# Attention's first keys and queries on two queues, one load per query tile, and Fourier weights in a work tile

## The chip, the core and the metric

The kernel runs on one core of a Trainium2 chip. The core has five engines, each with its own instruction queue: TensorE (PE, matmuls; the profile lists its weight loads as PEld), VectorE (DVE), ScalarE (ACT), GpSimd (POOL) and SyncE (SP). Instructions of one queue run in the order in which they are written there, and wait on semaphores for the other engines. DMAs are issued by SP, ACT or POOL. The metric is the device time of one execution in microseconds; lower is better.

## What is computed

The reference is a backbone of two layers on 2048 latent tokens and a prefix of 256 context tokens, 1024 wide. Each layer is one input projection that feeds four groups, and one output projection:

```python
hp = (rmsnorm(x, g) * (1 + scale) + shift) @ w_in
q  = (rmsnorm(hp[q]) @ w_uq) -> 4 heads x (64 plain + 32 rotary)
kn, kr, v = kv(hp[kv])           # kr: 32 rotary rows, shared by the 4 heads
s    = einsum("bqhd,bkhd->bhqk", q, concat(kn, kr)) / sqrt(96)
attn = softmax(s) @ v            # latents read latents and context: 2304 keys
four = real(fft2(hp[f], over tokens and within a group)) @ w_fourier + b_fourier
conv = conv_module(hp[c]);  sgu = spatial_gating(hp[s])
x = x + gate * (concat(attn, conv, four, sgu) * silu(hp[gate])) @ w_out
```

Context tokens go through the same weights in the first layer and give only keys and values in the second.

## The kernel before

Matmuls are done on fp32 data split into a high and a low part (names that end in h and l), so that one product is three matmuls: high x high (line 286), low x high (287), high x low (288). Keys and queries are kept in DRAM as such pairs between the stages.

A layer has three stages. **Phase A** projects the inputs, superblock by superblock of 768 tokens, each with its weights streamed through a ring (`ring<-wst`). `tm_a` makes the queries: `project()` computes two blocks of 128 plain rows and one block of 128 rotary rows of all heads, and `put` (line 522) splits each into two tiles called `th` and stores them on POOL. There are six `th` tiles, so the third put after one takes its tiles again. The Fourier branch is a generator that phase A advances a step at a time; it starts in the third superblock, multiplies the channel DFT by the weights `wf` (line 824), and reads its input `f` back from DRAM (`fx<-f`). Its weight tile came from its own pool, `fst`. Other short results live in three work tiles called `co`.

**Attention** works on two heads at a time over tiles of 256 queries. Its key tiles have 96 partitions: 64 plain rows of a head and the 32 shared rotary rows. `k0h`, `k0l` are those of the first head of a pair, `k1h`, `k1l` of the second, loaded in three chunks of 512, 768 and 1024 keys, with the plain and the rotary rows in a DMA each. A query tile `qh` or `ql` has 96 partitions too, filled by three DMAs. A score (`s<-k0h,qh`) is a 96-row matmul of 512 keys, in one of eight PSUM banks called s, t and o; DVE takes the maximum over the keys, ACT the exponential `e` (line 1014, with a table load first), and PE transposes `e` and multiplies it by `v`. **The output projection** follows.

The order of instructions on each engine is settled ahead by a scheduler; a load's place is that of its line in the program among the other instructions of its queue. Before attention, the program writes: the first query tiles of both heads on POOL, head 0's keys on POOL and head 1's on SP, the second query tiles on SP, and v on SP.

Of the kernel before, what the change touches and what calls it, by code (L numbers as in the profile page):

```python
# [16 lines left out]
F32 = mybir.dt.float32  # L17
# [7 lines left out]
P = 128  # L25
# [173 lines left out]
class Kern:  # L199
# [401 lines left out]
    def tm_a(self, l, seg, h, w, W, S):  # L601
        nc, A = self.nc, self.A
        t0, bw, cl0 = seg
        nt = bw // P
        lat = t0 < T
        full = not (l == L - 1 and not lat)
        c0 = 0 if full else 32
        kr = self.sq()[:, 0:96].rearrange("p (a b) -> p a b", b=32)
        held, cs = [], []

        def turn(t, cn):
            if t == 0:
                held.extend(self.bank("hold") for _ in range(2))
            for c in range(2):
                nc.tensor.transpose(held[c][:, t * P:(t + 1) * P], cn[:, c * P:(c + 1) * P], self.ident)
            if t == nt - 1:
                for c in range(2):
                    ch, cl = self.x("th", bw, F32R), self.x("th", bw, F32R)
                    self.split(held[c][:, :bw], ch, cl)
                    cs.append((ch, cl))  # L620
                self.later(LP, project)

        def key(krr):
            pk = self.bank("pj")
            for t in range(nt):
                nc.tensor.transpose(pk[0:32, t * P:(t + 1) * P], krr[:, t, :], self.ident)
            self.put(pk[0:32, :bw], [[(slice(0, 32), S["kr" + q][:, t0:t0 + bw])] for q in "hl"])

        def proj(m):
            ps = self.bank("pj")  # L630
            ms = slice(m * P, (m + 1) * P)
            self.mm3(ps[:, :bw], [(W["uq"][k][0][:, ms], W["uq"][k][1][:, ms], cs[k][0], cs[k][1])
                                  for k in range(2)])
            return ps[:, :bw]

        def project():
            for m in range(2):
                self.put(proj(m), [[(slice(0, P), S["q" + q][m * P:(m + 1) * P, t0:t0 + bw])] for q in "hl"])
            pr = proj(2)
            if lat:  # L640
                cos, sin, rot = (self.x("co", bw) for _ in range(3))
                nc.gpsimd.dma_start(out=cos, in_=A["cosq"][:, t0:t0 + bw])
                nc.gpsimd.dma_start(out=sin, in_=A["sinq"][:, t0:t0 + bw])
                for a, b in ((slice(0, 64), slice(64, P)), (slice(64, P), slice(0, 64))):
                    nc.scalar.copy(out=rot[b], in_=pr[a])
                nc.vector.tensor_tensor(cos, pr, cos, op=ALU.mult)
                nc.vector.tensor_tensor(rot, rot, sin, op=ALU.mult)
                nc.vector.tensor_tensor(cos, cos, rot, op=ALU.add)
                pr = cos
            self.put(pr, [[(slice(0, P), S["qr" + q][:, t0:t0 + bw])] for q in "hl"])  # L650

        for t in range(nt):
            ps = self.bank("mm")
            hs = slice(cl0 + t * P, cl0 + (t + 1) * P)
            self.mm3(ps[:, c0:288], [(h[k][0][:, hs], h[k][1][:, hs], w[k][0][:, c0:288], w[k][1][:, c0:288])
                                     for k in range(KT)])
            self.tick()
            nc.scalar.copy(out=kr[:, t], in_=ps[:, 256:288])
            if full:
                sq, ss, r, cn = self.junk(), self.st(), self.st(), self.sq()  # L660
                nc.scalar.activation(out=sq, in_=ps[:, 0:256], func=AF.Square, accum_out=ss[:, 0:1])
                nc.vector.tensor_scalar(ss[:, 1:2], ss[:, 0:1], 1.0 / 256, RMS_EPS, op0=ALU.mult, op1=ALU.add)
                self.rpow(r[:, :1], ss[:, 1:2])
                nc.vector.tensor_scalar(cn, ps[:, 0:256], r[:, 0:1], None, op0=ALU.mult)
                self.later(LT, lambda t=t, cn=cn: turn(t, cn))
        if lat:
            tb = self.sq().rearrange("p (a b c) -> p a b c", a=2, c=32)
            g0 = t0 // P
            nc.gpsimd.dma_start(out=tb[:, 0, :nt], in_=A["cosk"][:, g0:g0 + nt])
            nc.gpsimd.dma_start(out=tb[:, 1, :nt], in_=A["sink"][:, g0:g0 + nt])  # L670
            nc.vector.tensor_tensor(tb[:, 0, :nt], kr[:, :nt], tb[:, 0, :nt], op=ALU.mult)
            for a, b in ((slice(0, 16), slice(16, 32)), (slice(16, 32), slice(0, 16))):
                nc.vector.tensor_tensor(tb[:, 1, :nt, b], kr[:, :nt, a], tb[:, 1, :nt, b], op=ALU.mult)
            nc.vector.tensor_tensor(tb[:, 0, :nt], tb[:, 0, :nt], tb[:, 1, :nt], op=ALU.add)
            krr = tb[:, 0]
        else:
            krr = kr
        self.later(LT + 1, lambda: key(krr))
# [57 lines left out]
    def phase_a(self, l, xsrc, S, hcur, h0, lp, conv, w):  # L736
# [6 lines left out]
        for i, sb in enumerate(SBS):  # L743
# [20 lines left out]
            for ci, name in enumerate(CM_ORDER[i]):  # L764
                w = self.load_w(A["winC"][l, CM.index(name)], 256, lp)
                for seg in cmb:
                    self.lastseg = seg is cmb[-1]
                    self.cm(name, seg, hcur, w, S, M)
                if ci == 0 and i < 2:
                    hnext = self.norm_alloc((self.ap, h0)[i])  # L770
                    self.norm_sb(l, SBS[i + 1], xsrc, hnext)
                if ci == 0 and i == 2:
                    while self.dq:
                        self.tick()
                    self.h1x.__exit__(None, None, None)
                    self.npx.__exit__(None, None, None)
                    fx = self.pool(f"F{l}", "right")
                    steps = self.fourier(l, S, fx.__enter__())
                    self.every = lambda: [next(steps, None) for _ in range(2 if l < L - 1 else 3)]
                if name == "c1":  # L780
                    conv.avail(first + n if i < 2 else NTOK)
# [8 lines left out]
        self.ringx.__exit__(None, None, None)  # L790


    def fourier(self, l, S, p):


        nc, A, v = self.nc, self.A, self.v
# [4 lines left out]
        def T_(tag, shape, dt=F32, bufs=1):  # L801
            return self.t(p, tag, shape, dt, bufs)

        wf = T_("fst", [P, 512], bufs=2).rearrange("p (a b) -> p a b", b=256)
        nc.gpsimd.dma_start(out=wf, in_=A["wf"][l])
        altr, altc = T_("altr", [P, 512]), T_("altc", [P, 1])
        nc.gpsimd.dma_start(out=altr, in_=A["altr"].broadcast_to([P, 512]))
        nc.gpsimd.dma_start(out=altc, in_=A["altc"])
# [153 lines left out]
            yield  # L962


    def load_k(self, S, pool, pr):

        out = []
        for q in range(2):
            h = 2 * pr + q
            kk = [self.t(pool, f"k{q}{part}", [96, NTOK], F32R) for part in "hl"]  # L970
            for a, b in ((0, 512), (512, 1280), (1280, NTOK)):
                s = slice(a, b)
                for part, k in zip("hl", kk):
                    eng = self.nc.gpsimd if h == 0 else self.nc.sync
                    eng.dma_start(out=k[0:64, s].bitcast(F32), in_=S["k" + part][64 * h:64 * h + 64, s])
                    eng.dma_start(out=k[64:96, s].bitcast(F32), in_=S["kr" + part][:, s])
            out.append(kk)
        return out

    def load_q(self, S, pool, h, q0, eng):  # L980
        out = []
        for part in "hl":
            q = self.t(pool, "q" + part, [96, 256], F32R, 4)
            s = slice(q0, q0 + 256)
            eng.dma_start(out=q[0:64].bitcast(F32), in_=S["q" + part][64 * h:64 * h + 64, s])
            for a in range(2):
                r = slice(64 * a + 16 * h, 64 * a + 16 * h + 16)
                eng.dma_start(out=q[64 + 16 * a:80 + 16 * a].bitcast(F32), in_=S["qr" + part][r, s])
            out.append(q)
        return out  # L990

# [251 lines left out]

    def scratch(self, l):
        return {n: self.dr.tile(shape, F32, name=f"{n}{l}") for n, shape in (
            ("kh", [256, NTOK]), ("kl", [256, NTOK]), ("qh", [256, NTOK]), ("ql", [256, NTOK]),
            ("krh", [32, NTOK]), ("krl", [32, NTOK]), ("qrh", [P, NTOK]), ("qrl", [P, NTOK]),
            ("v", [P, NTOK // P, 256]), ("glu", [256, NTOK]), ("dw", [256, NTOK]), ("f", [256, NTOK]),
            ("ys", [256, NTOK]), ("g", [768, NTOK]), ("att", [256, NTOK]), ("conv", [256, NTOK]),
            ("four", [256, NTOK]))}  # L1250
# [1 line left out]
    def build(self):  # L1252
        tc, nc, A = self.tc, self.nc, self.A
        with ExitStack() as es:
# [37 lines left out]
            for l in range(L):  # L1292
# [11 lines left out]
                with self.pool(f"V{l}", "right") as vp:  # L1304
                    vt = self.t(vp, "v", [P, NTOK // P, 256])
                    k0 = self.pool(f"K0_{l}", "left")
                    k0p = k0.__enter__()
                    q0 = [self.load_q(S, k0p, q, 0, nc.gpsimd) for q in range(2)]
                    keys = self.load_k(S, k0p, 0)
                    q1 = [self.load_q(S, k0p, q, 256 if last else T, nc.sync) for q in range(2)]  # L1310
                    nc.sync.dma_start(out=vt, in_=S["v"][:, :, :])
                    self.psum(s=5, t=2, o=1)
                    nc.scalar.activation(out=self.st()[:, 0:1], in_=self.mhalf[:, 0:1], func=AF.Exp)
# [202 lines left out]
```

## Time and profile before

| what | us |
|---|---|
| three runs | 2959.75, 2963.6 (median), 2967.0 |
| the profiled execution | 2965.82 |
| its span, first to last instruction | 2963.8 |
| busy: PE, DVE, ACT, POOL | 2829.0, 1956.1, 1206.9, 569.2 |
| mean granted clock of PE, of full speed | 0.975 |

PE is busy in 95% of the span, so its idle stretches are few and each has a name. A busy time is not a bound by itself: matmuls at half clock count as busy too. In the views "idle before" is the time in which the engine stood just before an instruction, with what ended it.

### The profile page before, as it was taken

To read this page: it belongs to the slowest core of one execution; us is meant where nothing else is said; L and a number is where in the kernel's file an instruction comes from. 1 tells how busy PE (TensorE), PEld (TensorE's weight loads), DVE (VectorE), ACT (ScalarE), POOL (GpSimd) and SP (SyncE) were. 2 spreads that over 40 slices of the span, in tenths; PEclk is the share of its full clock that TensorE was granted. 3 is DMA by queue.
4 is the path that set the end of the run, shared out by engine and by line. 5 is a ranking of instruction groups with operands and counts; after the bars stand their busy time and mean duration, and the time that the engine had idled before them with its cause. 6 is when DMAs were issued, how large, how long until landed. Compare 5 with 4: busy or idle time off the path is not lost. (4 is left out here: it accounts for less than half of the span.)

```text
span 2963.8 us, 50552 instructions
## 1 busy us (share of the span) xinstructions
PE 2829.0 (95%) x18434; PEld 2429.3 (82%) x18434; DVE 1956.1 (66%) x4301; ACT 1206.9 (41%) x3228; POOL 569.2 (19%) x951
## 2 busy tenths in 40 slices
PE   6999999999699999999999999999979999999998
PEld 4889999899567777769998899998767777776998
DVE  5578488485377777654553695894827777775554
ACT  3432343433344454543322343343425455554432
POOL 2301311421211111112322212113321110011210
PEclk8999999999799999999999999999989999999999
DMA  7465343433521010016543443444453101000653
GB/s 244 139 194 177 107 132 106 161 123 117 163 56 29 29 48 25 21 30 207 182 153 117 157 158 105 137 136 139 148 164 93 33 22 45 18 28 15 187 155 110
DMA packets 221849, 326.75 MB, mean 110 GB/s; under 512 B 33456, under 2 KB 152752, under 8 KB 220832
## 3 DMA queue, kind: packets, MB, share of 16 engines
q1 hardware_dynamic: 191392, 240.66, 26.9%
q0 software_dynamic: 29776, 82.83, 8.3%
q8 instruction: 145, 2.38, 0.3%
q14 instruction: 104, 0.85, 0.1%
q10 hardware_dynamic: 432, 0.04, 0.0%
HBM read 232.30 MB, written 91.10 MB: 109 GB/s over the span
## 5 line engine op out<-in xcount | busy, mean ns | idle before, releaser
L1005 DVE TENSOR_REDUCE st<-s 128x1 f32<-128x512 f32 (+1 forms) x636 | 384.9, 631 | 184.4 <-PE s L288 182.6
L1014 ACT ACTIVATE e<-s,st 128x512 f32<-128x512 f32 (+1 forms) x636 | 399.4, 646 | 236.9 <-DVE st L1009 228.3
L286 PE MATMUL mm<-hh,ring 128*128 128x384 f32 (+1 forms) x1408 | 491.4, 349 | 0.0
L287 PE MATMUL mm<-hl,ring 128*128 128x384 f32 (+1 forms) x1408 | 484.7, 344 | 0.0
L288 PE MATMUL mm<-hh,ring 128*128 128x384 f32 (+1 forms) x1408 | 484.1, 344 | 0.0
L1451 DVE SCALAR_TENSOR_TENSOR acc<-win,c_cw,acc 128x384 f32<-128x384 f32 (+5 forms) x780 | 428.4, 572 | 7.4
L1035 PE MATMUL t<-ident,e 128*128 128x128 f32 x2320 | 341.8, 278 | 3.5 <-DVE et L1038 1.9
L1028 PE MATMUL o<-et,v 128*64 128x256 f32 x2320 | 343.7, 392 | 0.0
L1035 PEld LDWEIGHTS t<-ident,e 128*128 128x128 f32 x2320 | 259.7, 141 | 94.9 <-issue 43.7
L1038 DVE COPY et<-t 128x512 f32<-128x512 f32 x377 | 257.9, 686 | 92.1 <-PE t L1035 86.1
L286 PE MATMUL mm<-yh,woh 128*128 128x256 f32 x1040 | 297.2, 286 | 5.2 <-DVE xn L1223 3.7
L288 PE MATMUL mm<-yh,wol 128*128 128x256 f32 x1040 | 293.9, 283 | 0.2 <-DVE wol L278 0.2
L287 PE MATMUL mm<-yl,woh 128*128 128x256 f32 x1040 | 293.8, 282 | 0.1
L286 PEld LDWEIGHTS mm<-hh,ring 128*128 128x128 f32 x1408 | 267.8, 190 | 19.4 <-issue 9.5
L277 ACT CAST ring<-wst 128x256 fp32r<-128x256 f32 (+2 forms) x480 | 184.1, 418 | 240.2 <-DMA wst<-winC 125.4
L287 PEld LDWEIGHTS mm<-hl,ring 128*128 128x128 f32 x1408 | 267.9, 190 | 5.9
L288 PEld LDWEIGHTS mm<-hh,ring 128*128 128x128 f32 x1408 | 267.3, 190 | 5.8
L278 DVE TENSOR_TENSOR ring<-wst,ring 128x256 fp32r<-128x256 f32 (+2 forms) x480 | 201.2, 451 | 74.6 <-ACT ring L277 60.1
L1040 ACT COPY et<-t 128x512 f32<-128x512 f32 x203 | 119.1, 588 | 317.8 <-PE t L1035 317.6
L1028 PEld LDWEIGHTS o<-et,v 128*64 128x64 f32 x2320 | 153.1, 136 | 99.0 <-issue 51.9
L286 PEld LDWEIGHTS mm<-yh,woh 128*128 128x128 f32 x1040 | 198.4, 191 | 6.9 <-DVE xn L1223 4.3
L287 PEld LDWEIGHTS mm<-yl,woh 128*128 128x128 f32 x1040 | 198.3, 191 | 0.4 <-DVE yl L278 0.4
(319 smaller groups left out, 5284.8 us busy)
## 6 DMA issues: line engine op xcount, KB each, us to landing
wst<-winC SPq DMA_DIRECT2D x192, 256.0 KB, 3.1
ast<-wada SPq DMA_DIRECT2D x32, 512.0 KB, 4.5
gt<-g SPq DMA_DIRECT2D x102, 128.0 KB, 3.0
g<-co POOLq DMA_DIRECT2D x60, 192.0 KB, 2.2
wst<-winB SPq DMA_DIRECT2D x24, 384.0 KB, 3.4
x<-xn POOLq DMA_DIRECT2D x72, 128.0 KB, 2.8
ast<-wada SPq DMA_DIRECT2D x8, 1024.0 KB, 9.6
fst<-ft SPq DMA_DIRECT2D x32, 256.0 KB, 3.2
```

The lines of the kernel that those rows point to most:

```text
L277: a = self.nc.scalar.copy(out=hi, in_=src)
L278: b = self.nc.vector.tensor_tensor(lo, src, hi.bitcast(F32), op=ALU.subtract)
L286: mm(out, lhsT=lh, rhs=rh, start=start and i == 0, stop=False)
L287: mm(out, lhsT=lh, rhs=rl, start=False, stop=False)
L288: self.last = mm(out, lhsT=ll, rhs=rh, start=False, stop=stop and i == n - 1)
L1005: self.red = nc.vector.reduce_max(mx[:, i:i + 1], ps[:, :w], axis=AX.X)
L1014: nc.scalar.activation(out=e, in_=ps, func=AF.Exp, bias=nb[:, 0:1], accum_out=sm[:, i:i + 1])
L1028: nc.tensor.matmul(job.o[64 * q:64 * q + 64, 0:256], lhsT=vt[:, g, 64 * h:64 * h + 64], rhs=et[:, 256 * q:256 * q + 256], start=kt == 0, s ...
L1035: nc.tensor.transpose(ps[:, j * P:(j + 1) * P], job.es[j][kt], self.ident)
L1038: nc.vector.tensor_copy(et, ps)
L1040: nc.scalar.copy(out=et, in_=ps)
L1451: eng.scalar_tensor_tensor(ac, win[:, t:t + w], v["cw"][:, l, c, t:t + 1], ac, op0=ALU.mult, op1=ALU.add)
```

## The change

Queries are laid out in DRAM by head, 96 rows each, so that one DMA fills a query tile; the store of a rotary block becomes two DMAs per part, and the store of a plain block has a target of 2 x 64 rows. `load_k` and `load_q` take a list of queues: head 0's first query tile and its keys go with the high part on SP and the low part on ACT; head 1's first query tile and the second query tiles of both heads go on POOL. `wf` is loaded into a `co` tile ahead of the drain of the queued steps, not into the `fst` tile inside the generator.

```diff
 # tm_a, project()
-                self.put(proj(m), [[(slice(0, P), S["q" + q][m * P:(m + 1) * P, t0:t0 + bw])] for q in "hl"])
+                self.put(proj(m), [[(slice(0, P), S["q" + q][2 * m:2 * m + 2, 0:64, t0:t0 + bw])] for q in "hl"])
...
-            self.put(pr, [[(slice(0, P), S["qr" + q][:, t0:t0 + bw])] for q in "hl"])
+            self.put(pr, [[(slice(64 * a, 64 * a + 64), S["q" + q][:, 64 + 16 * a:80 + 16 * a, t0:t0 + bw])
+                           for a in range(2)] for q in "hl"])
 # phase_a
                 if ci == 0 and i == 2:
+                    wf = self.x("co", 512).rearrange("p (a b) -> p a b", b=256)
+                    self.nc.gpsimd.dma_start(out=wf, in_=A["wf"][l])
                     while self.dq:
                         self.tick()
...
-                    steps = self.fourier(l, S, fx.__enter__())
+                    steps = self.fourier(l, S, fx.__enter__(), wf)
 # fourier
-        wf = T_("fst", [P, 512], bufs=2).rearrange("p (a b) -> p a b", b=256)
-        nc.gpsimd.dma_start(out=wf, in_=A["wf"][l])
 # load_k
-                for part, k in zip("hl", kk):
-                    eng = self.nc.gpsimd if h == 0 else self.nc.sync
-                    eng.dma_start(out=k[0:64, s].bitcast(F32), in_=S["k" + part][64 * h:64 * h + 64, s])
-                    eng.dma_start(out=k[64:96, s].bitcast(F32), in_=S["kr" + part][:, s])
+                for i, part in enumerate("hl"):
+                    eng = engs[i] if engs else self.nc.sync
+                    eng.dma_start(out=kk[q][i][0:64, s].bitcast(F32), in_=S["k" + part][64 * h:64 * h + 64, s])
+                    eng.dma_start(out=kk[q][i][64:96, s].bitcast(F32), in_=S["kr" + part][:, s])
+            engs = None
 # load_q
-            eng.dma_start(out=q[0:64].bitcast(F32), in_=S["q" + part][64 * h:64 * h + 64, s])
-            for a in range(2):
-                r = slice(64 * a + 16 * h, 64 * a + 16 * h + 16)
-                eng.dma_start(out=q[64 + 16 * a:80 + 16 * a].bitcast(F32), in_=S["qr" + part][r, s])
+            engs[i % len(engs)].dma_start(out=q.bitcast(F32), in_=S["q" + part][h, :, q0:q0 + 256])
 # the layer's loop
-                    q0 = [self.load_q(S, k0p, q, 0, nc.gpsimd) for q in range(2)]
-                    keys = self.load_k(S, k0p, 0)
-                    q1 = [self.load_q(S, k0p, q, 256 if last else T, nc.sync) for q in range(2)]
+                    q0 = [self.load_q(S, k0p, q, 0, *((nc.sync, nc.scalar), (nc.gpsimd,))[q]) for q in range(2)]
+                    keys = self.load_k(S, k0p, 0, (nc.sync, nc.scalar))
+                    q1 = [self.load_q(S, k0p, q, 256 if last else T, nc.gpsimd) for q in range(2)]
```

Three places in the order of instructions show what moves. On SP at the end of layer 0's phase A, `four` is the last Fourier store of phase A; before, head 1's keys follow it.

```order
258 L961 DMA four_110<-fb_7604 128x256
259 L961 DMA four_110<-fb_7672 128x256
260 L975 DMA k1h_7829<-kh_94 64x512
261 L976 DMA k1h_7829<-krh_98 32x512
262 L975 DMA k1l_7830<-kl_95 64x512
```

With the change, seven rows stand ahead of them there.

```order
260 L984 DMA qh_7811<-qh_96 96x256
261 L975 DMA k0h_7819<-kh_94 64x512
262 L976 DMA k0h_7819<-krh_98 32x512
263 L975 DMA k0h_7819<-kh_94 64x768
264 L976 DMA k0h_7819<-krh_98 32x768
265 L975 DMA k0h_7819<-kh_94 64x1024
266 L976 DMA k0h_7819<-krh_98 32x1024
267 L975 DMA k1h_7821<-kh_94 64x512
268 L976 DMA k1h_7821<-krh_98 32x512
```

On ACT at the same place, the row of `co<-mm` is the activation of phase A's last matmul and the table load is that of the exponential; before, the table load follows directly. With the change, the low part of the first query tile and of the keys stands between.

```order
562 L720 ACTIVATE co_7797<-mm_7772 128x384
563 L984 DMA ql_7813<-ql_97 96x256
564 L975 DMA k0l_7820<-kl_95 64x512
565 L976 DMA k0l_7820<-krl_99 32x512
566 L975 DMA k0l_7820<-kl_95 64x768
567 L976 DMA k0l_7820<-krl_99 32x768
568 L975 DMA k0l_7820<-kl_95 64x1024
569 L976 DMA k0l_7820<-krl_99 32x1024
570 L1010 ACT_TABLE_LOAD
```

On POOL in layer 1's third superblock, before, the load of `wf` comes behind the last block's stores.

```order
747 L522 DMA qh_17353<-th_22758 128x256
748 L522 DMA ql_17354<-th_22759 128x256
749 L722 DMA f_17362<-co_22787 128x512
750 L522 DMA qrh_17357<-th_22781 128x256
751 L522 DMA qrl_17358<-th_22782 128x256
752 L522 DMA krh_17355<-th_22793 32x256
753 L522 DMA krl_17356<-th_22794 32x256
754 L805 DMA fst_22853<-wf 128x512
755 L807 DMA altr_22855<-altr 128x512
```

With the change, it stands ahead of the rotary stores, which are two rows per part, and `altr` (a constant of the Fourier branch) takes the place behind the stores.

```order
733 L522 DMA qh_17221<-th_22634 2x64x256
734 L522 DMA ql_17222<-th_22635 2x64x256
735 L775 DMA co_22668<-wf 128x512
736 L522 DMA qh_17221<-th_22657 4x16x256 x2
737 L522 DMA ql_17222<-th_22658 4x16x256 x2
738 L723 DMA f_17228<-co_22665 128x512
739 L522 DMA krh_17223<-th_22673 32x256
740 L522 DMA krl_17224<-th_22674 32x256
741 L808 DMA altr_22733<-altr 128x512
```

On PE in layer 1 the product with `wf` (`c_cd` is the channel DFT) stood, before, inside a block of eight weight pairs `hh`, `hl`.

```order
11091 L286 MATMUL mm_22887<-hh_4193_20616,ring_17377 128x512
11092 L287 MATMUL mm_22887<-hl_4194_20617,ring_17377 128x512
11093 L824 MATMUL hold_22873<-fst_22853,c_cd 128x256 x2
11094 L824 MATMUL hold_22880<-fst_22853,c_cd 128x256 x2
11095 L288 MATMUL mm_22887<-hh_4193_20616,ring_17377 128x512
```

With the change, it stands 20 matmuls earlier, between the end of one block and the first pair of the next.

```order
11071 L287 MATMUL mm_22708<-hl_4196_20493,ring_17243 128x512
11072 L288 MATMUL mm_22708<-hh_4195_20492,ring_17243 128x512
11073 L825 MATMUL hold_22751<-co_22668,c_cd 128x256 x2
11074 L825 MATMUL hold_22758<-co_22668,c_cd 128x256 x2
11075 L286 MATMUL mm_22765<-hh_4181_20478,ring_17243 128x512
```

## Rows read from the trace of the kernel before

**Rows 1.** PE's waits: engine, line, releaser; us in total, times, longest.

```profile
PE s L286 <- DMA k0l<-krl: 27.5, 2, 14.1
...
PE hold L824 <- DMA fst<-wf: 10.8, 2, 6.3
```

**Rows 2.** Timeline of PE, layer 0's attention start: start, us, engine, instruction, idle before.

```profile
764.21 0.77 PE L286 MATMUL s<-k0h,qh 96*128 96x512 f32 x1 [13.47 <-DMA k0l<-krl]
...
778.28 0.76 PE L287 MATMUL s<-k0l,qh 96*128 96x512 f32 x1 [6.53 <-DMA k0l<-krl]
```

**Rows 3.** Timeline of POOL, the same place.

```profile
752.18 1.00 POOL L988 DMA_DIRECT2D qh<-qrh  x2
...
757.65 0.54 POOL L975 DMA_DIRECT2D k0h<-kh  x1
```

**Rows 4.** Timeline of SP's queue, the same place.

```profile
738.87 0.33 SPq L961 DMA_DIRECT2D four<-fb  x1
750.81 0.52 SPq L975 DMA_DIRECT2D k1h<-kh  x1
```

**Rows 5.** Timeline of ACT at attention's start, layers 0 and 1.

```profile
751.34 1.28 ACT L1014 ACT_TABLE_LOAD   x1
781.61 0.69 ACT L1014 ACTIVATE e<-s,st 128x512 f32<-128x512 f32 x1 [28.99 <-DVE st L1009]
...
2194.63 1.28 ACT L1014 ACT_TABLE_LOAD   x1
2218.91 0.69 ACT L1014 ACTIVATE e<-s,st 128x512 f32<-128x512 f32 x1 [23.00 <-DVE st L1009]
```

**Rows 6.** Timeline of PE, layer 1's attention start.

```profile
2207.99 0.77 PE L286 MATMUL s<-k0h,qh 96*128 96x512 f32 x1 [14.05 <-DMA k0l<-krl]
```

**Rows 7.** Windows: us, busy (instructions) by engine, granted clock, DMA share, GB/s.

```profile
750.00:755.00 5.00, 0.74 (x5) 0.42 (x3) 0.00 (x0) 1.77 (x2) 3.39 (x7) 0.96 0.51 139
...
765.00:770.00 5.00, 4.76 (x11) 3.31 (x11) 1.25 (x2) 0.00 (x0) 1.00 (x2) 0.50 1.08 292
...
2065.00:2070.00 5.00, 5.00 (x23) 4.04 (x22) 1.48 (x4) 1.32 (x4) 2.60 (x5) 1.00 0.96 295
...
2195.00:2200.00 5.00, 0.00 (x0) 0.00 (x0) 0.00 (x0) 0.92 (x1) 5.00 (x10) 0.84 0.87 248
```

**Rows 8.** DMA issues in 750 to 770: KB each, median us to landing.

```profile
k1h<-kh SPq DMA_DIRECT2D x1, 256.0 KB, 5.2
...
k0l<-kl POOLq DMA_DIRECT2D x1, 256.0 KB, 9.3
...
k1h<-kh SPq DMA_DIRECT2D x1, 128.0 KB, 2.6
...
k0l<-kl POOLq DMA_DIRECT2D x1, 128.0 KB, 6.0
```

**Rows 9.** Timeline of PE at the products with wf, both layers.

```profile
593.15 2.05 PE L824 MATMUL hold<-fst,c_cd 128*128 128x256 f32 x4 [4.42 <-DMA fst<-wf]
...
600.35 1.02 PE L824 MATMUL hold<-fst,c_cd 128*128 128x256 f32 x4
...
2079.16 3.57 PE L824 MATMUL hold<-fst,c_cd 128*128 128x256 f32 x8 [6.34 <-DMA fst<-wf]
```

**Rows 10.** Timeline of POOL ahead of wf, layer 0 and layer 1.

```profile
578.81 0.57 POOL L722 DMA_DIRECT2D f<-co  x1 [2.43 <-ACT co L716]
...
2063.52 0.54 POOL L522 DMA_DIRECT2D ql<-th  x1
2065.24 0.54 POOL L722 DMA_DIRECT2D f<-co  x1 [1.18 <-ACT co L716]
...
2075.21 0.57 POOL L805 DMA_DIRECT2D fst<-wf  x1 [7.37 <-DMA qrl<-th]
```

**Rows 11.** DMA issues in 2058 to 2070.

```profile
f<-co POOLq DMA_DIRECT2D x1, 256.0 KB, 8.3
```

**Rows 12.** DMA issues of the whole span, and ACT's timeline in phase A.

```profile
qh<-th POOLq DMA_DIRECT2D x16, 192.0 KB, 3.2
...
572.85 0.37 ACT L277 CAST th<-hold 128x256 fp32r<-128x256 f32 x1 [0.24 <-DMA qh<-th]
```

More of the change, by code (lines that the diff above doesn't have):

```diff
@@ L790, in phase_a, with fourier @@
         self.ringx.__exit__(None, None, None)
-    def fourier(self, l, S, p):
+    def fourier(self, l, S, p, wf):
         nc, A, v = self.nc, self.A, self.v
@@ L962, in fourier, with load_k, load_q @@
             yield
-    def load_k(self, S, pool, pr):
-        out = []
+    def load_k(self, S, pool, pr, engs=None):
+        kk = [[self.t(pool, f"k{q}{part}", [96, NTOK], F32R) for part in "hl"] for q in range(2)]
         for q in range(2):
             h = 2 * pr + q
-            kk = [self.t(pool, f"k{q}{part}", [96, NTOK], F32R) for part in "hl"]
             for a, b in ((0, 512), (512, 1280), (1280, NTOK)):
                 s = slice(a, b)
-                for part, k in zip("hl", kk):
-                    eng = self.nc.gpsimd if h == 0 else self.nc.sync
-                    eng.dma_start(out=k[0:64, s].bitcast(F32), in_=S["k" + part][64 * h:64 * h + 64, s])
-                    eng.dma_start(out=k[64:96, s].bitcast(F32), in_=S["kr" + part][:, s])
-            out.append(kk)
-        return out
-    def load_q(self, S, pool, h, q0, eng):
+                for i, part in enumerate("hl"):
[3 more added lines that the diff above has]
+            engs = None
+        return kk
+    def load_q(self, S, pool, h, q0, *engs):
         out = []
-        for part in "hl":
+        for i, part in enumerate("hl"):
             q = self.t(pool, "q" + part, [96, 256], F32R, 4)
-            s = slice(q0, q0 + 256)
-            eng.dma_start(out=q[0:64].bitcast(F32), in_=S["q" + part][64 * h:64 * h + 64, s])
-            for a in range(2):
-                r = slice(64 * a + 16 * h, 64 * a + 16 * h + 16)
-                eng.dma_start(out=q[64 + 16 * a:80 + 16 * a].bitcast(F32), in_=S["qr" + part][r, s])
+            engs[i % len(engs)].dma_start(out=q.bitcast(F32), in_=S["q" + part][h, :, q0:q0 + 256])
             out.append(q)
@@ L1245, in scratch @@
         return {n: self.dr.tile(shape, F32, name=f"{n}{l}") for n, shape in (
-            ("kh", [256, NTOK]), ("kl", [256, NTOK]), ("qh", [256, NTOK]), ("ql", [256, NTOK]),
-            ("krh", [32, NTOK]), ("krl", [32, NTOK]), ("qrh", [P, NTOK]), ("qrl", [P, NTOK]),
+            ("kh", [256, NTOK]), ("kl", [256, NTOK]), ("qh", [H, 96, NTOK]), ("ql", [H, 96, NTOK]),
+            ("krh", [32, NTOK]), ("krl", [32, NTOK]),
             ("v", [P, NTOK // P, 256]), ("glu", [256, NTOK]), ("dw", [256, NTOK]), ("f", [256, NTOK]),
```

## The prediction

> **What bounds the kernel now.** I read the waits of TensorE (PE) first, since PE is the engine that is never done: they ask where it stands still and for whom. Two of the costliest belong to the change: 27.5 us for the low key tile of head 0 (k0l), twice, and 10.8 us for the Fourier weights (wf), twice [rows 1]. The timeline says where. In layer 0 the first score matmul starts at 764.21 after 13.47 us of standing, so phase A's last matmul ended at 750.74; it stands again for 6.53 us before 778.28, for the same tile [rows 2]. In layer 1 it stands for 14.05 us before 2207.99 [rows 6]. Both wf waits are 4.42 and 6.34 us [rows 9].
>
> Why k0l is late is read on the queue that issues it. POOL begins on the query pieces at 752.18 and reaches the first key row only at 757.65 [rows 3]: twelve query pieces of half a us stand ahead of it, and its key rows alternate h and l. Meanwhile SP is free from 738.87 and, from 750.81, loads head 1's keys, which are needed later [rows 4]. So this is a stage bound by the order of issues, and only then by transfers (292 GB/s, with the DMA engines' share at 1.08 in 765 to 770) [rows 7].
>
> **The change part by part, attention's start.** Behind SP's store of 738.87 now stand qh and head 0's six k0h rows. Their waits in the order are for weight tiles and matmuls long done, so they are issued some 12 us before phase A ends, and I count them as landed. The l half goes to ACT, behind the activation of the last matmul; there ACT was free at 751.34 and 2194.63 [rows 5]. No row shows a DMA issued from ACT; the bounds are nothing and SP's 0.52 us [rows 4], and POOL's 0.54 [rows 3]. I take 0.5: ql at 751.34, k0l's first two rows done issuing by 752.3.
>
> When does the first chunk land? A row of 128 KB took 2.6 us on the emptier queue's first issues and 6.0 in the crowd [rows 8]. I take 3 after 751.84, that is 754.9, since the order lets only SP's first k1 row run beside it: the second k1 row counts its landing on the semaphore that k0l's third row uses and waits for that row to land. The bounds are 754.4 and 757.8. ACT's 64x1024 row waits likewise for the first chunk, so it goes out at 754.9; 256 KB took 5.2 to 9.3 us [rows 8], and at 5.2 it lands at 760.1.
>
> From first score to first exponential layer 1 took 2218.91 - 2207.99 = 10.92 us, with PE at half clock and no long wait [rows 5, 6]. With that pace layer 0's first exponential is at 754.9 + 10.9 = 765.8, against 781.61: **15.8 us** earlier. In layer 1 ACT's first chunk goes out at 2195.1 and lands at 2198.1; the exponential follows at 2209.0 against 2218.91: **9.9 us**. What comes after (twenty exponentials, then the steady loop) is unchanged, so this is carried to the end. With the first chunk at its late bound each loses 2.9.
>
> ACT's seven issues and their waits put the table load for Exp at about 756 instead of 751.34; ACT had nothing until 781.61, and still has nothing until 765.8, so this costs nothing; without that cover it would be some 4.5 us a layer. SP's 248 fewer rows are query loads inside the loop, and none of PE's large waits names one: nothing. V moves up behind k1; it is needed after the exponentials: nothing.
>
> **Fourier weights.** In layer 0 wf moves up to just ahead of the f store of 578.81 [rows 10]. Even at the 8.3 us that the slowest 256 KB store of that kind took [rows 11] it lands by 588, before PE stops at 588.73. The 4.42 us go, and so does half clock behind it: the four L824 matmuls took 2.05 us, and 1.02 at full clock [rows 9]. **5.4 us.** In layer 1 the gain is smaller. wf goes out between POOL's store of 2063.52 and that of 2065.24 [rows 10], beside the 1 MB of fx; the 256 KB issued at 2065.24 took 8.3 us [rows 11]. So from 2064.6 wf lands at about 2072.9. But the scheduler now places its matmuls 20 places earlier, and 23 matmuls take 5 us there [rows 7]: they come up at 2072.82 - 20 x 0.22 = 2068.4 and wait 4.5 us instead of 6.34. **1.8 us**, with bounds of 0 (a later landing) and 6.3 (landing in the 3.95 us from 2075.21 to 2079.16 [rows 9, 10]).
>
> **Query stores.** Each of the 13 calls of project() issues two more DMAs on POOL, 0.54 us each, 14 us in all beside an engine that idles most of the time. The th tiles come free later, though, and there the cover is thin: ACT already waited 0.24 us at 572.85 for a query store to land [rows 12]. This, the work tile that wf holds and the next wait that a PE that is ahead will meet I put at **3 us** together; the bounds are 0 and the rival below.
>
> The sum: 15.8 + 9.9 + 5.4 + 1.8 - 3 = 29.9 us. The profiled execution took 2965.8 us (span 2963.8), so 2935.9; it lies 2.2 above the median of the runs, so **2933.7 us**.
>
> Here is a rule to weigh. Before 757.65 nothing held k0l but POOL's rows [rows 3]. The Trainium skill (DMA: Bandwidth & Descriptors, "Issuing engines are not separate DMA queues") says that DMAs of all issuing engines share the same 16 DMA engines, so that spreading them saves issue time alone. By that rule the three-queue spread gains only the issue time; [rows 3, 4] show that here this is about 6 us of POOL and the 12 us of SP's start, which the sum takes.
>
> **The rivals.**
> - *PE's clock stays up.* The mean granted clock of 0.96 in 750 to 755 and 0.84 in 2195 to 2200 [rows 7] puts its fall from 2.4 to 1.2 GHz at 3.9 and 4.5 us after the last matmul. The gap would now be about 4.2 us with one score matmul in it. If the clock stays, the last chunk decides: 760.1 plus half of the 3.33 us from 778.28 to 781.61 [rows 2, 5] gives 761.8; in layer 1 2203.3 + 1.7 = 2205.0. That is 8.0 more: 2926. Against it: the gap is not clearly shorter.
> - *Transfers in the way.* k0l shares the engines with k1 and the queries, as k0l's rows did at 6.0 and 9.3 us [rows 8]. The first chunk at 757.8 and the same in layer 1 costs 5.8; with store delays of half a us per call (6.5) the time is 2946.
> - *Query stores on few DMA engines: slower than before.* The stores of 192 KB landed in 3.2 us [rows 12]. Their target is now written as 2 blocks of 64 rows, and as 4 of 16 for the rotary rows. If such a store ran on two of the 16 engines, at 292/16 = 18 GB/s each [rows 7] it would take 5.4 us for the data instead of 0.7, and land in about 8. ACT's cast of the third put after it has no slack [rows 12], and ACT feeds PE's weights in order. At 3 us of PE per call, 13 calls cost 39 us: 2933.7 + 39 = 2973. It decides from 2.3 us per call. No row before has such a target, so nothing in the trace speaks for or against the two engines; many matmuls of other blocks lie between the puts, which speaks against PE seeing it all. The Trainium skill (DMA: Bandwidth & Descriptors, "Why a DMA increments its semaphore by 16 and not by 1") has the rule: the number of engines is the largest up to 16 that divides the slowest dimension of both sides, which would be 2 and 4 here, with an exception for some copies issued from GpSimd. No run here shows it yet.
> - *Nothing moves.* SP's k0h rows could be held until phase A ends by memory that isn't free. The order speaks against it (the matmul that they wait for is of the last query projection). Then the l half, on ACT, would still go first, and only the wf gain and little else came: about 2960.
>
> **How the numbers follow.** My forecast 0.50, the clock 0.15, transfers and stores in the way 0.21, nothing 0.05, stores slower 0.09. A measurement of this kernel can tell about 0.2% (6 us) from no change. Faster by more than that: 0.50 + 0.15 + 0.21 = 0.86; same 0.05; slower 0.09. The range reaches to the clock's case with wf's early landing and the 3 us unspent (2926 - 4.5 - 3, and 4 for half clock that is not paid after it: 2914) and to the crowded case with another 8 us of stores (2954); it leaves out the last two and a little of each side.
>
> **What would show it.** Right: first scores with k0l near 755 and 2198, first exponentials near 766 and 2209; no wait for wf in layer 0 and one of some 4 us in layer 1, on the new wf tile; SP's k0h rows right behind 738.87. Wrong: a first exponential past 772; query stores landing in 6 us or more with ACT waiting for them through phase A; new PE waits on th or on ring tiles of over 10 us in all.

## The result, and the profile after

The changed kernel takes 2998.34 us (median of four runs, 2991.65 to 2999.71) against 2961.68 for the kernel before in the same session: a ratio of 1.0117, 95% interval [1.0095, 1.0139]. It is slower by about 35 us; forecast was 2933.7.

The five stages are read from windows that are cut at phase A's last matmul and at the last exponential of each layer: us; then busy time of PE, PEld, DVE, ACT and POOL; PE's granted clock; DMA share; GB/s. The last stage, the output projection of layer 1, is not shown. Before:

```profile
0.00:750.74 750.74, 706.48 (x4318) 661.43 (x4318) 498.56 (x1142) 273.26 (x700) 171.90 (x294) 0.97 0.46 149
750.74:1307.20 556.46, 529.39 (x3357) 378.92 (x3356) 392.38 (x833) 272.75 (x774) 73.53 (x131) 0.97 0.18 51
1307.20:2193.90 886.70, 853.37 (x5610) 800.83 (x5608) 547.86 (x1212) 315.31 (x803) 223.00 (x365) 0.99 0.46 143
2193.90:2719.10 525.20, 509.74 (x3273) 368.92 (x3272) 387.73 (x803) 266.02 (x753) 65.05 (x115) 0.97 0.17 49
```

After, cut at the same events:

```profile
0.00:783.60 783.60, 714.64 (x4319) 667.08 (x4319) 502.64 (x1142) 272.11 (x700) 190.47 (x308) 0.95 0.46 144
783.60:1328.90 545.30, 528.31 (x3359) 378.79 (x3359) 392.39 (x834) 273.13 (x774) 64.42 (x113) 0.98 0.17 50
1328.90:2229.80 900.90, 858.48 (x5609) 805.25 (x5605) 546.63 (x1212) 315.40 (x803) 240.87 (x377) 0.98 0.46 142
2229.80:2753.10 523.30, 511.56 (x3272) 370.65 (x3271) 387.03 (x803) 266.37 (x753) 56.02 (x97) 0.97 0.16 47
```

Attention became shorter, by 11.2 and 1.9 us. The stages with a phase A became longer, by 32.9 and 14.2. With the last stage (244.7 to 244.8) that is 34.1 us, the difference of the spans (2963.8 to 2997.9). In layer 0's phase A, PE's standing grew from 44.3 to 69.0 us (window less busy time); its busy time grew by 8.2 us with the same matmuls, while the granted clock fell from 0.97 to 0.95. In the stage with layer 1's phase A it is 9.1 us of standing and 5.1 of busy time (clock 0.99 to 0.98).

**Where phase A lost.** The DMA issues of the whole span show the query stores (KB each, median us to landing):

```profile
qh<-th POOLq DMA_DIRECT2D x16, 192.0 KB, 9.6
ql<-th POOLq DMA_DIRECT2D x16, 192.0 KB, 12.5
qh<-th POOLq DMA_DIRECT2D x16, 96.0 KB, 9.3
ql<-th POOLq DMA_DIRECT2D x16, 96.0 KB, 8.8
```

The first kind landed in 3.2 us before [rows 12], the second (`ql`) in 3.7; the last two are the rotary stores, which landed in 2.2 and 2.4 us before, with 192 KB in one DMA. The waits of all engines show what that holds up (us in total, times, longest):

```profile
DVE th L278 <- DMA ql<-th: 49.3, 18, 6.8
...
PE pj L286 <- DVE th L278: 36.6, 17, 5.3
ACT th L277 <- DMA qh<-th: 35.5, 15, 7.9
```

So ACT and DVE, which write the `th` tiles, wait for the stores that read them, and PE waits for `th`. Before, the waits of ACT and DVE for these stores (the rotary ones included) came to 1.4 and 0.8 us, and the one of PE to a third:

```profile
PE pj L286 <- DVE th L278: 12.7, 9, 3.7
```

One such place after the change, on ACT:

```profile
127.65 0.48 ACT L277 CAST th<-hold 128x384 fp32r<-128x384 f32 x1 [0.26 <-DMA qh<-th]
136.06 0.48 ACT L277 CAST th<-hold 128x384 fp32r<-128x384 f32 x1 [7.93 <-DMA qh<-th]
137.45 0.47 ACT L277 CAST th<-pj 32x384 fp32r<-32x384 f32 x1 [0.91 <-DMA qh<-th]
```

PE's next stands are at 139.68 and 145.72, of 1.70 and 4.18 us, both for `th`. In the chain of work that ended last, followed back from the last instruction, landings of query stores now are steps of their own (start, us, step):

```profile
1664.89 8.29 DMA ql<-th
...
1877.15 12.84 DMA ql<-th
```

Transfers beside them land later too. In the stretch 118 to 135, two 512 KB loads on SP and the rotary cosine's load on POOL (KB, median us to landing; before, 5.8 for the one such load there, and 3.7):

```profile
ast<-wada SPq DMA_DIRECT2D x2, 512.0 KB, 10.7
...
co<-cosq POOLq DMA_DIRECT2D x1, 192.0 KB, 11.5
```

Over the whole span the cosine's loads of 192 KB went from 3.7 to 6.8 us, the 512 KB loads only from 4.5 to 4.8.

**Attention's start.** PE, layer 0; the first score is at 783.56, right behind phase A:

```profile
788.16 0.77 PE L287 MATMUL s<-k0l,qh 96*128 96x512 f32 x1 [4.21 <-DMA k0l<-krl]
...
792.44 0.79 PE L287 MATMUL s<-k0l,qh 96*128 96x512 f32 x1 [1.81 <-DMA k0l<-krl]
...
802.06 0.39 PE L288 MATMUL s<-k1h,ql 96*128 96x512 f32 x1
803.92 0.50 PE L286 MATMUL o<-k1h,qh 96*128 96x512 f32 x1 [1.48 <-ACT e L1010]
...
809.63 0.64 PE L286 MATMUL s<-k1h,qh 96*128 96x512 f32 x1 [1.62 <-ACT e L1010]
```

And ACT at the same place:

```profile
783.89 0.35 ACTq L984 DMA_DIRECT2D ql<-ql  x1
...
788.82 1.28 ACT L1010 ACT_TABLE_LOAD   x1 [4.52 <-DMA k0l<-krl]
798.62 0.69 ACT L1010 ACTIVATE e<-s,st 128x512 f32<-128x512 f32 x1 [8.51 <-DVE st L1005]
...
808.80 0.69 ACT L1010 ACTIVATE e<-s,st 128x512 f32<-128x512 f32 x1 [3.80 <-DVE st L1005]
```

The last matmul of phase A ends at 783.73 (the windows cut 0.1 before it), and the first exponential comes 14.9 us later instead of 30.9 (layer 1: 15.4 instead of 25.0). PE's waits for k0l were 27.5 us in the two of [rows 1] and 6.8 in two more; 12.0 in four are left. But from the first to the last exponential the loop takes 530.4 us instead of 525.6 (798.62 to 1328.97; before, 781.61 to 1307.23), and in layer 1 508.0 instead of 500.2: 4.7 and 7.8 us are given back, in the first passes with head 1's keys, where PE now waits for ACT's `e` (11.2 us in ten instead of 4.9 in seven, over the whole span).

**Fourier weights.** No wait in layer 0, and in layer 1:

```profile
2111.43 3.78 PE L825 MATMUL hold<-co,c_cd 128*128 128x256 f32 x8 [6.84 <-DMA co<-wf]
```

### The profile page after: what moved, and what is told of

It reads as the page before. It is cut to its first block, busy times and chain, and to the rows that moved or that the text cites. A ratio compares the mean times of both kernels' runs of the same rounds, so it can differ in the third digit from the quotient of the medians.

```text
span 2997.9 us, 50169 instructions
## 1 busy us (share of the span) xinstructions
PE 2842.7 (95%) x18434; PEld 2440.7 (81%) x18434; DVE 1960.4 (65%) x4301; ACT 1206.7 (40%) x3228; POOL 586.4 (20%) x941
## 4 chain that ended last, share of the span: by engine, by line
PE 65%; DVE 5%; DMA 5%; issue 2%; ACT 2%; POOL 1%; SPq 0%; POOLq 0%; DVEq 0%; ACTq 0%
PE o L1024 10%; PE t L1031 9%; PE mm L286 9%; PE mm L288 8%; PE mm L287 8%; PE s L286 5%; PE s L288 4%; PE s L287 4%; DVE acc L1447 1%; DMA wst<-winC 1%; DMA ql<-th 1%; PE hold L288 1%; PE hold L287 1%; PE hold L286 1%; ACT e L1010 1%
## 5 line engine op out<-in xcount | busy, mean ns | idle before, releaser
L288 PEld LDWEIGHTS mm<-yh,wol 128*128 128x128 f32 x1040 | 197.3, 190 | 1.4 <-DVE wol L278 1.3
```

Of the source, the lines that this page charges most:

```text
L288: self.last = mm(out, lhsT=ll, rhs=rh, start=False, stop=stop and i == n - 1)
```

## The experiments

Three questions: which part of the change costs the 47 us of phase A, by what mechanism, and why attention keeps only half of its start. Ratios are to the kernel before in the same session; 1% is 29.6 us.

**The order alone** (the changed kernel with the query layout, stores and three-piece loads of before):

```diff
-    S["q" + q][2 * m:2 * m + 2, 0:64, t0:t0 + bw]      # plain stores
+    S["q" + q][m * P:(m + 1) * P, t0:t0 + bw]
-    engs[i % len(engs)].dma_start(out=q.bitcast(F32), in_=S["q" + part][h, :, q0:q0 + 256])
+    ...                                                # three DMAs, on the same queue
```

> The changed kernel with the old layout of the queries: stores of 128 rows, query tiles in three DMAs; the queues of the first loads and the place of wf stay changed. Theory, the query stores land late because their target is written as 2 or 4 blocks and the data then goes through few DMA engines: without them phase A has its old length, the first exponentials come 16.0 and 9.6 us earlier as they did in the changed kernel, of which 4.4 and 7.8 are lost again at head 1, and wf gives some 6: 2935 to 2945 us, query stores landing in 2 to 4 us. Rival, the new queues or the work tile of wf cost the time: 2975 us or more, with stores that land in 2 to 4 us all the same.

2942.02 us, ratio 0.9951 [0.993, 0.9971]. The plain stores land in 3.2 and 3.6 us again and phase A loses nothing (in layer 0 its last matmul ends at 740.43, before at 750.74). But the loop takes 531.7 and 507.1 us from first to last exponential, 6.1 and 6.9 over before: the loss in head 1's ramp belongs to the order, not to the layout.

**The layout alone** (the kernel before, with the new layout, stores and one load per query tile):

> The kernel before with only the new layout of the queries: target of 2 x 64 and 4 x 16 rows, one DMA per query tile; queues and wf as before. Theory (late query stores): phase A is longer by 40 to 60 us, 3000 to 3022 us, stores landing in 7 to 13 us. Rival (new queues or wf): within 10 us of the kernel before, 2952 to 2972.

3006.01 us, 1.0159 [1.0138, 1.018]: 47 us, more than the whole slowdown. With the order's -0.5% it adds up to the changed kernel's +1.2%.

**The plain stores' target alone** (before, with the same number of DMAs; the rotary rows stay as they were):

```diff
-    self.put(proj(m), [[(slice(0, P), S["q" + q][m * P:(m + 1) * P, t0:t0 + bw])] for q in "hl"])
+    self.put(proj(m), [[(slice(0, P), S["q" + q][2 * m:2 * m + 2, 0:64, t0:t0 + bw])] for q in "hl"])
...                                                    # in load_q, the same rows by their new place
-    ("qh", [256, NTOK])
+    ("qh", [H, 96, NTOK])
```

> The kernel before with only the plain query rows kept in a DRAM tensor of 4 x 96 rows, so that their store has a target of 2 x 64 rows; as many DMAs as before, of the same bytes; rotary rows and loads in three DMAs as before. Theory, the blocks of the target decide: plain stores land in 7 to 12 us against 3.2, rotary ones near 3 unless they queue behind, time 2985 to 3010 us. Rival, it is the number of DMAs and POOL's time to issue them: stores land in 3 to 4 us and the time is within 6 us of before.

3007.12 us, 1.0162 [1.0142, 1.0181]: as much as the whole layout, with no DMA more. The stores by kind (KB, median us to landing):

```profile
qh<-th POOLq DMA_DIRECT2D x16, 192.0 KB, 8.9
ql<-th POOLq DMA_DIRECT2D x16, 192.0 KB, 11.1
qrh<-th POOLq DMA_DIRECT2D x8, 192.0 KB, 8.5
```

The rotary stores, unchanged, took 8.5 us instead of 2.2, behind the plain ones on POOL's queue. So the two more DMAs a call and their issue time, which the prediction counted, are not what costs, nor are the query tiles loaded by one DMA; the target written as 2 x 64 is.

**All stores in pieces** (the changed kernel; plain stores of 64 rows, rotary stores of 16: 24 DMAs a call instead of 8):

```diff
-    [(slice(0, P), S["q" + q][2 * m:2 * m + 2, 0:64, t0:t0 + bw])]
+    [(slice(64 * b, 64 * b + 64), S["q" + q][2 * m + b, 0:64, t0:t0 + bw]) for b in range(2)]
...                                      # rotary stores
-    for a in range(2)]
+    for a in range(2) for b in range(4)]
```

> The changed kernel with each query store cut into pieces whose target is one block: two DMAs of 64 rows for a plain block, eight of 16 rows for a rotary block, per part; 24 DMAs per call of project() in place of 8. Theory (blocks of the target): the pieces land in 2 to 4 us and phase A shortens in spite of 16 more issues of half a us each, 2940 to 2970 us. Rival (number of DMAs and POOL's issue time): slower than the changed kernel, over 3005 us.

2953.33 us, 0.9978 [0.9964, 0.9992]: three times as many DMAs, and 1.4% faster than the changed kernel. The pieces land in 2.8 us (96 KB) and 1.8 us (24 KB).

**Plain stores in pieces** (the same, with the rotary stores left as 4 x 16):

> The changed kernel with each plain store cut into two DMAs of 64 rows, the rotary stores left as 4 x 16 rows. By theory A the rotary stores, with 4 blocks, are still slower than the 16-row pieces (1.8 us in the run with all stores cut, ratio 0.9978): 3 to 6 us, and the time lies between that run and the changed kernel, 2950 to 2975. By theory B too the rotary stores are slow, some 8 us as in the changed kernel: 2970 to 2990.

2957.25 us, 0.9992 [0.9983, 1.0001], within the first range. The plain pieces of 96 KB land in 2.8 us (high part) and 3.1 (low part), the rotary stores of 4 x 16 rows, also 96 KB, in 3.7 and 4.5, as theory A had it. Two DMAs in place of one for each plain part take back the slowdown against the kernel before. They don't reach the order alone (0.9951): some 12 us of the layout are left here, and some 8 with all stores in pieces (0.9978, with an interval that meets the other).

**Sixteen blocks** (the kernel before, plain rows in 16 blocks of 8 with gaps, the same number of DMAs and bytes):

```diff
-    S["q" + q][m * P:(m + 1) * P, t0:t0 + bw]
+    S["q" + q][16 * m:16 * m + 16, 0:8, t0:t0 + bw]
-    in_=S["q" + part][64 * h:64 * h + 64, s]
+    in_=S["q" + part][8 * h:8 * h + 8, 0:8, s]
...
-    ("qh", [256, NTOK])
+    ("qh", [32, 12, NTOK])
```

> The kernel before, with only the plain query rows stored into blocks with gaps again, as in the run with 2 x 64 (1.0162), but into 16 blocks of 8 rows, with the same number of DMAs and bytes and 64-row loads that read 8 blocks of 8. Theory A, the number of blocks sets how many DMA engines work on a store: with 16 blocks a store of 192 KB lands in 3 to 4 us as before, and the time is within 0.4% of before. Theory B, any target that is not one run of rows is slow: it lands in 8 us or more and the time is 30 to 50 us over before.

2965.21 us, 1.0027 [1.0017, 1.0038]. The stores land as before:

```profile
qh<-th POOLq DMA_DIRECT2D x16, 192.0 KB, 3.1
ql<-th POOLq DMA_DIRECT2D x16, 192.0 KB, 3.2
```

A target in blocks is not slow in itself; one of two blocks is. PE's waits for `th` (line 286) go with it: 33.0 us with plain targets of 2 x 64 and 34.2 with the whole layout, but 17.2 with 16 blocks, 17.8 and 21.1 with the stores in pieces, and 12.7 before.

How many DMA engines work can be read from windows of the first superblock's query stores. The changed kernel, where the four plain stores were issued from 120.71 to 124.08 and the first data moved at 122.1:

```profile
120.00:125.00 5.00, 3.94 (x23) 3.94 (x24) 2.85 (x6) 1.85 (x5) 3.24 (x4) 1.00 0.15 24
122.00:124.00 2.00, 2.00 (x14) 2.00 (x13) 1.14 (x3) 1.16 (x3) 1.87 (x3) 1.00 0.23 34
```

And the kernel with 16 blocks, its plain stores issued from 118.48 to 121.38:

```profile
120.00:125.00 5.00, 5.00 (x35) 4.40 (x33) 2.69 (x5) 3.10 (x5) 2.43 (x5) 1.00 0.53 162
```

A DMA share of 0.15 is 2.4 of 16 engines, at 24 GB/s; with 16 blocks it is 8.5 engines and 162 GB/s (rotary stores and a load that follow in those 5 us included). The single packets of the trace say it without these. From 122.5 to 124.0, while only the first store's data moved, 2.0 data packets were under way at a time, and 4.0 to 4.1 from 124.5 to 126.5, when the second's had begun; in the kernel before it was 15 during such a store (123.5 to 124.0). Most data packets have 4608 bytes in all three kernels, so it is not that the data went in smaller packets. The changed kernel has 1344 packets of 12 bytes beside them in 120.5 to 135; at 9 ns each they come to 12 us, spread over 16 engines. The 34 GB/s of 122 to 124 are 17 for each of two engines (the prediction took 18). The Trainium skill (DMA: Bandwidth & Descriptors, "Why a DMA increments its semaphore by 16 and not by 1") gives the number of engines as the largest up to 16 that divides the slowest dimension of both sides. The trace agrees: 8.9 to 12.5 us to land where that is 2, and 3.1 where it is 16; the exception for some copies from GpSimd, which the prediction named, did not apply to these stores. The 8 us that are left (0.27%) have no cause found; the 64-row loads of 8 x 8 blocks are the only other edit.

**The Fourier weights alone:**

```diff
+    wf = self.x("co", 512).rearrange("p (a b) -> p a b", b=256)
+    self.nc.gpsimd.dma_start(out=wf, in_=A["wf"][l])
-    wf = T_("fst", [P, 512], bufs=2).rearrange("p (a b) -> p a b", b=256)
-    nc.gpsimd.dma_start(out=wf, in_=A["wf"][l])
```

> The kernel before with the Fourier weights' edit alone (a co tile, loaded ahead of the drain). My theory: the wait of 4.42 us in layer 0 goes and some of the 6.34 us in layer 1 (the kernel with the order of loads kept still waited 3.7 us there), so the first exponentials come 4 to 10 us earlier in layer 0 (in that kernel phase A's last matmul came 10.3 us earlier, more than 5.4) and the time is 5 to 13 us shorter, 2948 to 2956. Rival: the co tile that wf holds is missed elsewhere, so that what the wait gives is paid back on other waits: within 3 us of before.

2961.0 us against 2962.34, 0.9991 [0.9978, 1.0004]: the rival, though the interval still reaches a gain of 6.5 us. The waits did shrink, from 10.8 us in two to 4.0 in one, and the time is shorter by less than the measurement can tell. PE's largest other wait in phase A grew from 12.7 to 15.6 us:

```profile
PE pj L286 <- DVE th L278: 15.6, 11, 3.9
...
PE hold L824 <- DMA co<-wf: 4.0, 1, 4.0
```

**The first loads' queues alone** (the kernel before; `load_k` and `load_q` on lists of queues):

> The kernel before with the new queues for attention's first loads alone (queries in three pieces, Fourier weights as before). My theory: the first exponential comes 14 to 17 us earlier in layer 0 and 9 to 12 us in layer 1, and some 4 and 7 us of that are lost again in head 1's ramp, so the time is 10 to 15 us shorter: 2946 to 2951. Rival (the prediction's): the start is carried to the end whole, 25.7 us: 2935.

2950.71 us, 0.9954 [0.9939, 0.997], or 13.6 us, as my theory of that moment had it: half of the 25.7 that the start gains. It equals the order alone (0.9951), which has the Fourier edit too. From first to last exponential the loop is 8.2 and 6.6 us longer than before.

**Head 1's keys on POOL** (the order alone, with head 1's first keys on POOL and the second query tiles on SP):

```diff
-    keys = self.load_k(S, k0p, 0, (nc.sync, nc.scalar))
-    q1 = [self.load_q(S, k0p, q, 256 if last else T, nc.gpsimd) for q in range(2)]
+    keys = self.load_k(S, k0p, 0, (nc.sync, nc.scalar), nc.gpsimd)   # head 1 on POOL
+    q1 = [self.load_q(S, k0p, q, 256 if last else T, nc.sync) for q in range(2)]
```

> The kernel with the old layout and the new order (2942.0), but with head 1's keys on POOL and the second query tiles on SP, so that head 1's keys no longer stand on SP behind the landings of the k0l rows. If the loss of 4 and 7 us in head 1's ramp comes from keys that are late: 5 to 11 us faster than that kernel, 2931 to 2937, and the ramp loss gone. If it comes from PE running ahead of ACT, standing, and then running at half clock: within 3 us of 2942, and the same drop of the granted clock behind the first exponentials.

2938.88 us, 0.9915 [0.9893, 0.9936]. This lies just outside both stated ranges: by the ratios it is some 10 us below the order alone, by the medians 3.1, and the two intervals overlap, so this pair alone does not decide. The loop speaks for a gain: it takes 529.3 and 501.0 us, 3.7 and 0.8 over before, instead of 6.1 and 6.9. Yet PE waited for no key of head 1 in either kernel. What differs is PE's own order. With the keys on SP, layer 0, order alone:

```profile
757.68 0.50 PE L286 MATMUL s<-k1h,qh 96*128 96x512 f32 x1
...
758.49 0.40 PE L286 MATMUL s<-k1h,qh 96*128 96x512 f32 x1
...
758.96 0.40 PE L288 MATMUL s<-k1h,ql 96*128 96x512 f32 x1
760.82 0.50 PE L286 MATMUL o<-k1h,qh 96*128 96x512 f32 x1 [1.46 <-ACT e L1014]
```

and ACT's first exponential of head 1:

```profile
767.10 0.69 ACT L1014 ACTIVATE e<-s,st 128x512 f32<-128x512 f32 x1 [5.21 <-DVE st L1009]
```

With the keys on POOL:

```profile
766.61 0.50 PE L286 MATMUL s<-k1h,qh 96*128 96x512 f32 x1
...
768.10 0.39 PE L286 MATMUL s<-k1h,qh 96*128 96x512 f32 x1
768.40 0.51 PE L286 MATMUL t<-k1h,qh 96*128 96x512 f32 x1
...
770.45 0.40 PE L286 MATMUL o<-k1h,qh 96*128 96x512 f32 x1
```

```profile
771.87 0.69 ACT L1014 ACTIVATE e<-s,st 128x512 f32<-128x512 f32 x1 [1.05 <-DVE st L1009]
```

The chunk in bank `o` belongs to the second 128 queries. With the keys on SP it stands third, ahead of three chunks of the first 128 queries, and waits until ACT has read bank `o`; the maximum over the first 128 queries' keys comes late, and ACT stands. From head 1's first score to its first exponential it takes 9.42 us (757.68 to 767.10) instead of 5.26 (766.61 to 771.87); in layer 1 9.43 instead of 6.55. In the kernel before that chunk stood sixth too, and the same stretch of layer 0 took 6.21 us, in part at half clock. No run changes PE's order and leaves the queues as they are, so that the order is the cause is read from these waits and not shown by itself.

**PE kept busy** (the order alone, with one added score matmul per chunk in each layer's first query tiles, overwritten by the next):

```diff
+            if job.p == 0 and job.q0 == 0:
+                nc.tensor.matmul(ps[:, :w], lhsT=qq[0][:, qs], rhs=kk[0][:, a:a + w], start=True, stop=True)
```

> The kernel with the old layout and the new order (2942.0), with one more score matmul (high x high, into the same bank, overwritten by the one behind it) for each chunk in the first query tile of head 0 and of its pairs' ramps: about 10 extra matmuls of 0.4 to 0.8 us per pass, 4 to 8 us a pass if PE were the bound there. If PE's standing and the fall of the granted clock are what costs the 4 and 7 us: the clock stays near 1.00 behind the first exponentials, the shift of the exponentials is kept through the ramp, and the time is 2 to 8 us below 2942. If the loss has another cause, the added matmuls only cost: 2942 to 2955.

2945.08 us, 0.9941 [0.9921, 0.9961], not to be told from the order alone. The granted clock stayed up behind the first exponential at 762.37, where the order alone, with its first exponential at 755.51, fell to 0.66 in 760.5 to 765.5:

```profile
762.00:767.00 5.00, 3.99 (x19) 2.70 (x17) 4.22 (x10) 4.55 (x14) 0.00 (x0) 1.00 1.04 361
767.00:772.00 5.00, 4.13 (x19) 3.45 (x20) 0.44 (x1) 1.94 (x8) 0.00 (x0) 1.00 0.73 274
```

Still the loop gave back 6.4 and 6.1 us, of which head 1's ten added matmuls of 0.23 us can make 2.3. PE's order is that of the order alone, with a wait of 1.16 us at the same `o` chunk. So the fall of the clock is not the main cause; its own share could not be separated from the added work.

**Head 1's keys on POOL, Fourier weights as before:**

> The kernel with the new queues for the first loads alone (ratio 0.9954), with head 1's keys on POOL and the second query tiles on SP, Fourier weights as before. My theory: what head 1's ramp lost came from PE's order, which the scheduler wrote with the first chunk of the second 128 queries (in bank o) ahead of the rest of the first 128, because it counted head 1's keys on SP as late; on POOL that order is not written, and the gain of the start is kept: 5 to 10 us below that kernel, ratio 0.991 to 0.9935. If the difference between the two earlier kernels was chance: within 3 us of it, ratio 0.9945 to 0.9965. If the Fourier weights' edit is worth what the prediction took (7.2 us), it is also some 7 us slower than the kernel that has both (ratio 0.9915).

2933.45 us against 2959.13, 0.9909 [0.9892, 0.9927]: the fastest, a hair past its stated range, level with the kernel that has both edits (0.9915), and below the loads alone (0.9954) by 13 us, with intervals that don't meet. The loop takes 529.3 and 499.2 us, 4.6 and 7.6 less than with the loads alone, which is nearly all of it, and the `o` chunk stands sixth again (third with the loads alone). So the gain of POOL holds in a second pair, and the Fourier edit is worth nothing that can be measured.

## Why the prediction was wrong, point by point

- **Query stores: the step that failed.** The prediction put the two more DMAs, the freed `th` tiles, the work tile and the next wait at 3 us together, and gave 0.09 to the rival in which the stores run on two engines. That rival is what happened: landing forecast at about 8 us, measured 8.9 to 12.5; 39 us, measured 47 for the layout or the plain target alone. Its point from which it decides, 2.3 us a call, was passed: 47/13 = 3.6. The prediction's own signs of being wrong came true too: stores over 6 us, ACT waiting for them (35.5 us), and over 10 us of new waits for `th`. The reason against it, that many matmuls of other blocks lie between the puts, was never held against the six `th` tiles: one call of `project()` takes all six, ACT had no slack at 572.85 [rows 12], and the next call found them taken. Of the 47 us in the changed kernel, 34 are more standing of PE and 13 more busy time at a lower clock (24.7 + 9.1 and 8.2 + 5.1 in the windows above); its waits for `th` in lines 286 and 615 grew by 28. What transfers delayed beside the stores (10.7 us for 512 KB) add stays open.
- **Attention's start: right, in part by luck.** 15.8 and 9.9 us forecast; 16.0 and 9.6 measured. The key tile's first chunk released PE 4.4 us after phase A's end, forecast 4.2; SP's k0h rows went out right behind the last Fourier store (772.29, phase A's end at 783.73); the clock fell in the gap (0.59 in 785 to 790, 0.50 in 790 to 795). The pace from there was forecast as 10.9 us at half clock with no long wait, and 10.5 were measured; but they hold a second stand of 1.81 us for k0l (792.44) that was not forecast, and the clock was back at 0.88 in 795 to 800: the luck is that the two roughly cancel. Three slips change nothing: of the twelve query pieces eleven stood behind 752.18 (the first went out at 748.22); ACT's first three issues at 0.5 us end at 752.8 and not 752.3; and the early bound of layer 1's wf gain is 6.2 and not 6.3.
- **"What comes after ... is unchanged, so this is carried to the end": wrong.** 4.7 and 7.8 us are given back. The prediction saw that SP's second k1 row is held (783.75, then 791.46) and called the keys "needed later". On the chip they were not late; but PE's order had been written differently, and that was to be seen ahead, on PE's list of instructions. Putting head 1's keys on POOL brings the `o` chunk back to the sixth place and undoes most of the loss. That the scheduler wrote this order because it counted those keys as late is an inference; only the order and the stretch behind it were seen. The 3.7 us that layer 0 still gives back have no cause found.
- **Fourier weights: a mis-sized term.** 5.4 + 1.8 us forecast, 2.7 [-1.2, 6.5] measured for the edit alone (from its ratio), and no difference in the two other pairs. The layer 0 wait went, and with stores of 128 rows the layer 1 wait came down to 3.7 to 4.2 us, where 4.5 was forecast; in the changed kernel it stayed at 6.84, since wf, issued right behind four query stores, took 10.4 us to land and not 8.3. So the waits were forecast about right and their worth was not. What a removed wait gives was taken as time of the kernel, and PE met the next one.
- **The other rivals.** The clock that stays up did not come; "nothing moves" neither; and transfers in the way did not hold the first chunk to its late bound (7.1 us after phase A's end, measured 4.4). The forecast sum was -29.9: of it the start was right (25.6), 12.5 of it was given back, and phase A added 47.1, where the prediction had -4.2.

## What to carry to other kernels

A store's target is part of its cost: where a new layout turns one run of 128 rows into two blocks, look at the DMA share and the landing of that store (here 3.2 to 9 us and more), and cut it into one DMA per block or give it 16 blocks, which left 0.3 to 0.4% of the time as its cost here; more DMAs were far cheaper than slow ones. A buffer ring that is refilled every call turns a longer landing into a stall of whoever writes it, so hold the new landing time against the ring before calling it covered. When loads change queues under a scheduler, compare the order of the engine that consumes them, not only that of the queues; and a wait that goes is worth only what the next wait leaves.

## What the runs showed of the hardware

- A store of 192 KB from 128 partitions, issued on POOL, had 2.0 data packets under way at a time with a target of 2 x 64 rows, and 15 with one of 128 rows; it landed in 8.9 to 12.5 us instead of 3.2 to 3.7, and with 16 x 8 rows in 3.1 to 3.2.
- With plain stores of 2 x 64 rows alone, what stands behind them on the same queue lands later, though its own shape is unchanged: rotary stores 8.5 us instead of 2.2. In the first superblock loads on SP's queue do too, 512 KB 10.5 us (10.7 in the changed kernel) instead of 5.8.
- Issuing a store of 2 x 64 rows held POOL for 0.80 to 0.84 us in the first superblock (120.71 to 123.28), one of 128 rows for 0.54 to 0.55 at the same place before, one of 16 x 8 rows for 0.53 to 0.55.
- The same bytes of query stores cost less in 24 DMAs a call (0.9978) than in 8 (1.0117).
